# A fused diffusion layer on one core: the order of stores, casts and copies around the merged projections, changed in five places

## The chip, the core and the metric

The kernel runs on one core of a Trainium2 chip. The core has a matrix engine (TensorE, here PE; its weight loads are listed as PEld), three engines for elementwise work (VectorE, DVE; ScalarE, ACT; GpSimd, POOL) and SyncE (SP), which here only issues DMAs. POOL issues DMAs too. Each engine runs its own instructions in order and waits for the others by semaphores. The metric is the time of one execution on the device in microseconds, the median over runs.

## What is computed

One layer over 1024 latent tokens of width 1024, with 256 context tokens that only give the start states of a linear-attention scan. The reference, cut to what the change touches:

```
def project(h, w_in, w_a_up, b_a):
    z = h @ w_in
    q, k, v, g, lr_f, lr_b, u, bg, cg, r_gla, r_conv = jnp.split(z, offs, axis=-1)
...
def token_mixer(proj, grid_rows, s0_f, s0_b, gla_norm_g, gla_w_o, conv_w, conv_w_out, merge_w_out):
    o = o_f + flip_seq(o_b)                      # gated linear attention, two directions, 4 heads
    o = rms_norm(o, gla_norm_g).transpose(0, 2, 1, 3).reshape(bsz, n, GLA_DV).astype(dt)
    y_gla = (o * jax.nn.silu(g)) @ gla_w_o
    cu = cg * u
    conv = centred_conv3(cu.reshape(bsz, grid_rows, GRID_W, CONV_CH), conv_w).reshape(bsz, n, CONV_CH)
    y_conv = (bg * conv) @ conv_w_out
    merged = jax.nn.sigmoid(r_gla) * y_gla + jax.nn.sigmoid(r_conv) * y_conv
    return merged @ merge_w_out, s_f, s_b
...
    x = x + gt1 * y
    h = modulate(rms_norm(x, norm2_g[i]), sh2, sc2)
    x = x + gt2 * expert_choice_ffn(h, router_w[i], exp_w_gate[i], exp_w_up[i], exp_w_down[i])
return rms_norm(x, final_g)
```

The layer is followed by nothing else: 16 experts, each of which picks 128 of the 1024 tokens, take the second half of the time.

## The kernel before, in words

Matrices are in fp32, and a product of two of them is made of three matmuls in the engine's faster fp32r form: each operand is split into a high part (a cast on ACT, L75, names ending in h or hi) and a low part (a subtraction on DVE, L76, names ending in l or lo). In `mmw` (L88 is its matmul) the high and mixed terms of all rows come first, the terms with the weights' low part last.

**Heads and gates.** For each of four heads the kernel computes decays, values, queries and keys, and the scan (`head_core`, a generator), whose steps stand between the blocks of gate products (`gates`: four weights of two blocks each; ACT's sigmoid on L736 writes the block as `sgm`, and POOL stores it). The head's output `o` (two tiles) is then normed: DVE scales its eight pieces in place (L829), PE transposes them (L750, 16 of 128x128 a head), ACT copies the result (`ogs`, L752), and POOL stores it in `og_d`. This is `scale_store`. It is put on a list, `late`, and run in the next head behind its first values; for the last head it runs after the first of two weights of u products (`pu0`, two blocks each). `lm` makes the modulation of the second half meanwhile on DVE and PE (L768, L775). After `pu0` the pools of this part are closed, and the pools of the next part take over their space.

**Pairs.** The input projections u, cg, bg and g, two weight blocks of 128 columns at a time, are 15 "pairs" (`pair`; the first u is `pu0`): 2x2 blocks of weights and of tokens multiplied by seven products instead of eight, so that some operands are sums. A product is 12 matmuls into one PSUM bank; running sums are built up in the banks and copied out in between (`keep`, which calls `snap`, ACT, L953; 59 such copies). The token sums come from `tokens_split`: SP loads 16 pieces `yq` from DRAM (L869), four to a step k; each step has DVE's four sums (L879 and behind it) and two splits, and later two splits more, t3 and t4, the latter into the place of the old tokens. The weight sums come from `weights_side`, four steps to a pair: `whole(a)`, `whole(s_)`, then the differences, then `w3`; `whole` writes `whi` and `wlo` (three buffers each, the same ones that the gates' weights use). The pairs run u, cg, bg in turn (the first is cg), then four of G. `finish` of a cg pair adds, multiplies with u, and starts the conv over rows of 64: a multiply by the centre tap on ACT (L1052, `cv`) and two multiply-adds on DVE (L1054 is the first). `finish` of a bg pair multiplies and stores in `cv_d`. `finish` of a G pair takes the silu on ACT, multiplies by the head output loaded from `og_d` (`ot`) on DVE (L1077), and POOL stores it (L1078).

**Order.** From the token splits to the end of the last pair the order on PE, ACT and DVE is that of the code (`tc.manual_schedule`). What is to be done beside the products stands in a list `behind`: `prod` issues its 12 matmuls and then everything on that list, in the order in which it was put there. So a finish that was put there before a snapshot runs ahead of it on ACT. DMA queues (SP, POOL) and all that lies outside the stretch are ordered by the framework's scheduler, as is the program before it.

**Behind the pairs.** `cv_load` brings the conv rows back (16 tiles `cvt`, on POOL, L1089, from `cv_d`, each split into `cvh` and `cvl`): four ahead of the last pair, the others behind it, a load and its split at a time. The products with conv_w_out (24 matmuls each, `w` from a stream, operands `cvh`, `cvl`) follow the last pair at once. `t2_` tiles (128x512) of snapshots, `ot`, `cvt`, `cv`, `u` and `yq` share 14 buffers. The list `behind` is emptied like this:

```
        def prod(p, a, b, first=True):
            mmw(p, [(A[a](k), tk(b)(k)) for k in range(4)], 0, first, True, not first)
            for f in behind[:]:
                f()
            behind.clear()
```

Of the kernel before, what the change touches and what calls it, by code (L numbers as in the profile page):

```python
# [8 lines left out]
F32 = mybir.dt.float32  # L9
# [6 lines left out]
OP = mybir.AluOpType  # L16
# [19 lines left out]
def block_kernel(ctx: ExitStack, tc, x, c, cx, c_ctx, w_ada, b_ada, norm1_g, norm2_g, w_in, w_a_up, b_a,  # L36
# [717 lines left out]

    mod_d = dram.tile([4, D], F32, name="mod_d")
# [25 lines left out]
    for h in range(H):  # L781
# [6 lines left out]
        for t2 in range(0 if h else 2, 4):  # L788
            if t2 == 2:
                vt[1] = g4("v1")  # L790
            value_block(wv, vt, t2)
            drain(hd, 1)
            if t2 == 0 and late:
                late.pop()()
            if h:
                drain(lm, 1)
# [22 lines left out]
        drain(core, 1)  # L819
        while not drain(gt, 1):  # L820
            drain(core, 1)
            drain(lm, 1)
        drain(core)
        rs = small.tile([128, NCH], F32, name="rs_o", tag="rs_o")
        rstd_of(rs, ssq, DV, NCH)
        def scale_store(f, h=h, o=o, rs=rs):
            for t in range(4 * f, 4 * f + 4):
                os_ = o[f][:, (t % 4) * 256:(t % 4 + 1) * 256]
                V.tensor_scalar(os_, os_, rs[:, t:t + 1], None, op0=OP.mult)  # L829
            og_store(h, o, f)  # L830

        late.append(lambda f_=scale_store: (f_(0), f_(1)))
# [3 lines left out]
    for i in range(2):  # L836
        w = ws.get()
        for f in range(2):
            pu0[i, f] = p = ps()
            mmw(p, [(w(k), hs(k, f * 512, (f + 1) * 512)) for k in range(KT)])  # L840
        if late:
            late.pop()()
# [97 lines left out]
    def pair(n, finish, t_first=False):  # L940
# [4 lines left out]
        def prod(p, a, b, first=True):  # L945
            mmw(p, [(A[a](k), tk(b)(k)) for k in range(4)], 0, first, True, not first)
            for f in behind[:]:
                f()
            behind.clear()

        def snap(p, name="snap"):
            t = t2_(name)
            S.copy(t, p)  # L953
            return t

        def later(f):
            behind.append(f)

        def step():
            later(lambda: drain(nxt_, 1))  # L960
# [3 lines left out]
        def keep(n_, p):  # L964
            later(lambda: t.update({n_: snap(p)}))

        b1, b2, b3 = ps(), ps(), ps()
        if not t_first:
# [15 lines left out]
            later(lambda: finish(0, 1, b3, t["u2"]))  # L984
            prod(b1, (2, 2), (0, 1), False)
            step()
            later(lambda: finish(1, 0, b1, None))
# [6 lines left out]
        prod(b1, "s3", 3, False)  # L994
        prod(b2, (1, 1), (0, 0))
        keep("p1", b2)
        prod(b3, "s4", (1, 1), False)

# [21 lines left out]
    w0 = weights_side(0, ops[0])  # L1020
    drain(ts, 4)
    drain(w0, 1)
# [24 lines left out]
    def fin_cg(jp):  # L1047
        def finish(i, f, p, s_):
# [3 lines left out]
            S.activation(cvt, u, AF.Copy, scale=vcol("conv", 8 + j))  # L1052
# [12 lines left out]
    def fin_g(jp):  # L1065
# [5 lines left out]
        def finish(i, f, p, s_):  # L1071
            if s_ is not None:
                V.tensor_tensor(s_, p, s_, op=OP.add)
                p = s_
            sg = s_ if s_ is not None else t2_("sgg")
            S.activation(sg, p, AF.Silu)
            V.tensor_tensor(sg, sg, ot[i, f], op=OP.mult)  # L1077
            nc.gpsimd.dma_start(og2_d[2 * jp + i, :, f * 512:(f + 1) * 512], sg)  # L1078
# [4 lines left out]
    def cv_load():  # L1083
        for f in range(2):
            for g in range(2):
                hi, lo = cvT[g][f] = (Y("cvh"), Y("cvl"))
                for k in range(4):
                    t = t2_("cvt")
                    nc.gpsimd.dma_start(t, cv_d[4 * g + k, :, f * 512:(f + 1) * 512])  # L1089
                    split(hi[:, k * 512:(k + 1) * 512], lo[:, k * 512:(k + 1) * 512], t)  # L1090
                    yield
# [11 lines left out]
    for f in behind:  # L1103
        f()
# [655 lines left out]
```

## Time and profile before

| what | value |
| --- | --- |
| median of 3 runs | 2359.76 us (2357.66 to 2361.66) |
| profiled execution, its own time | 2357.01 us |
| its span in the profile | 2355.2 us (1.81 us lie around it) |
| PE busy | 2256.1 us, 96% |
| DVE busy | 1725.3 us, 73% |
| ACT busy | 1350.6 us, 57% |
| POOL busy | 281.2 us, 12% |
| heads and gates, u blocks | up to about 594 us |
| pairs | about 606 to 923 us |
| conv products, output products | from 923 us |

The page splits the span in 40 slices and gives PE's busy share in each: 9 tenths or more in 36 of them, 6 in the first, the fourteenth and the twenty-first, 7 in the last; its granted clock is at full speed in nearly all. Busy times are shares of one execution: an engine with 57% can still be the one that PE waits for at a certain place. The waits table names, for each idle stretch of an engine, what released it last. A timeline gives instructions by start time; several of one kind in a row are one row with their count. A matmul's time in such a row includes the end of its pipeline, so that neighbours overlap: the step from one start to the next is what it costs.

### The profile page before, as it was taken

Reading aid. Unit: us, or ns where it says so; the run is one execution under the profiler, and the core shown is the slowest. Engines: PE = TensorE matmul, PEld = TensorE weight load, DVE = VectorE, ACT = ScalarE, POOL = GpSimd, SP = SyncE. Lnnn points to the kernel's source line nnn. Section 1 sums busy time; section 2 is a strip of 40 time slices with the busy share of each in tenths; the row PEclk is TensorE's granted clock in tenths of the full one; section 3 lists DMA queues with packets and bytes.
Section 4 is the critical chain, followed back from the end, with each engine's and each line's share of the span. In section 5 each row is a group of like instructions: output and inputs, shape, how many; then the busy total and the mean of one; then the engine's idle time right before and its main releaser. Section 6 shows DMA issues by size and latency. Waiting matters only on the chain. (4 is left out here: it accounts for less than half of the span.)

```text
span 2355.2 us, 28981 instructions
## 1 busy us (share of the span) xinstructions
PE 2256.1 (96%) x10930; PEld 1866.7 (79%) x10930; DVE 1725.3 (73%) x2167; ACT 1350.6 (57%) x1554; POOL 281.2 (12%) x388
## 2 busy tenths in 40 slices
PE   6999999999699999999969999999999999999997
PEld 4888888888578777888748888888888888888885
DVE  5764545452855555458478999999999999999988
ACT  4744242422433334244328777778777777777786
POOL 1201010101000013420210110100111000011104
PEclk9999999999899999999989999999999999999998
DMA  9423333332322247765668999999999999999995
GB/s 324 147 69 109 109 104 101 116 93 86 101 68 66 72 139 232 242 192 168 254 224 310 374 379 377 384 389 389 385 380 380 386 373 399 386 387 383 375 349 212
DMA packets 356342, 589.60 MB, mean 250 GB/s; under 512 B 15499, under 2 KB 122097, under 8 KB 356201
## 3 DMA queue, kind: packets, MB, share of 16 engines
q1 hardware_dynamic: 331664, 506.65, 60.2%
q0 software_dynamic: 24192, 80.86, 10.3%
q8 instruction: 85, 1.39, 0.2%
q14 instruction: 57, 0.46, 0.1%
q10 hardware_dynamic: 344, 0.24, 0.0%
HBM read 537.34 MB, written 50.35 MB: 250 GB/s over the span
## 5 line engine op out<-in xcount | busy, mean ns | idle before, releaser
L76 DVE TENSOR_TENSOR ewl<-eraw,ewh 128x2048 fp32r<-128x2048 f32 (+1 forms) x391 | 865.2, 2222 | 93.6 <-ACT ewh L75 89.8
L75 ACT CAST ewh<-eraw 128x2048 fp32r<-128x2048 f32 (+1 forms) x391 | 726.7, 1862 | 224.0 <-PE ps L88 220.2
L88 PE MATMUL ps<-ewh,xeh 128*128 128x512 f32 x1024 | 404.5, 395 | 0.3 <-ACT xeh L75 0.3
L88 PE MATMUL ps<-ewh,xel 128*128 128x512 f32 x1024 | 399.8, 390 | 0.0
L88 PE MATMUL ps<-ewl,xeh 128*128 128x512 f32 x1024 | 274.0, 389 | 0.0
L88 PE MATMUL ps<-ewh,hd 128*128 128x512 f32 x1024 | 259.7, 396 | 0.0
L88 PE MATMUL ps<-hTh,whi 128*128 128x512 f32 x596 | 239.1, 401 | 11.9 <-ACT whi L75 11.9
L88 PE MATMUL ps<-hTl,whi 128*128 128x512 f32 x596 | 233.3, 391 | 0.0
L88 PEld LDWEIGHTS ps<-ewl,xeh 128*128 128x128 f32 x1024 | 192.2, 188 | 40.3
L88 PEld LDWEIGHTS ps<-ewh,xeh 128*128 128x128 f32 x1024 | 192.8, 188 | 39.3 <-ACT xeh L75 0.7
L88 PEld LDWEIGHTS ps<-ewh,xel 128*128 128x128 f32 x1024 | 192.9, 188 | 38.9 <-DVE xel L76 0.2
L88 PEld LDWEIGHTS ps<-ewh,hd 128*128 128x128 f32 x1024 | 189.7, 189 | 37.9
L75 ACT CAST whi<-wraw 128x1024 fp32r<-128x1024 f32 (+1 forms) x97 | 87.6, 917 | 155.9 <-PE ps L88 119.6
L76 DVE TENSOR_TENSOR wlo<-wraw,whi 128x1024 fp32r<-128x1024 f32 (+1 forms) x97 | 101.3, 1057 | 90.3 <-ACT whi L75 46.6
L88 PE MATMUL ps<-hTh,wlo 128*128 128x512 f32 x596 | 153.0, 391 | 0.0
L88 PEld LDWEIGHTS ps<-hTh,whi 128*128 128x128 f32 x596 | 112.7, 189 | 39.9 <-ACT whi L75 12.3
L88 PE MATMUL ps<-ewl,hd 128*128 128x512 f32 x512 | 137.4, 390 | 0.0
L1637 POOL DMA_INDIRECT x_d<-ye,idc x15 | 50.7, 3382 | 693.2 <-DVE ye L1636 693.2
L88 PEld LDWEIGHTS ps<-hTh,wlo 128*128 128x128 f32 x596 | 112.0, 189 | 23.7
L88 PEld LDWEIGHTS ps<-hTl,whi 128*128 128x128 f32 x596 | 112.7, 189 | 22.4
L88 PEld LDWEIGHTS ps<-ewl,hd 128*128 128x128 f32 x512 | 96.4, 188 | 20.5
L953 ACT COPY snap<-ps 128x512 f32<-128x512 f32 x59 | 34.5, 585 | 84.9 <-PE ps L88 84.9
(464 smaller groups left out, 3558.8 us busy)
## 6 DMA issues: line engine op xcount, KB each, us to landing
eraw<-in_exp_w_down_dram SPq DMA_DIRECT2D x128, 1024.0 KB
eraw<-in_exp_w_gate_dram SPq DMA_DIRECT2D x127, 1024.0 KB
eraw<-in_exp_w_up_dram SPq DMA_DIRECT2D x127, 1024.0 KB
wraw<-in_w_in_dram SPq DMA_DIRECT2D x76, 512.0 KB
raw<-in_w_ada_dram SPq DMA_DIRECT2D x64, 256.0 KB
adaw<-in_w_ada_dram SPq DMA_DIRECT2D x16, 512.0 KB
sig_d<-sgm POOLq DMA_DIRECT2D x32, 256.0 KB, 2.5
sgl<-sig_d POOLq DMA_DIRECT2D x32, 256.0 KB, 5.3
```

What stands on the lines that cost most here:

```text
L75: S.copy(hi, src)
L76: V.tensor_sub(lo, src, hi.bitcast(F32))
L88: T.matmul(p, a, b, start=first and i == 0, stop=last and i == len(seq) - 1, skip_group_check=again)
L953: S.copy(t, p)
L1637: nc.gpsimd.indirect_dma_start(out=x1_d[:, :], out_offset=bass.IndirectOffsetOnAxis(ap=idc[:, :1], axis=0), in_=ye, in_offset=None, comput ...
```

## The change

1. `scale_store` becomes a generator, `head_out`: the norm's factors and the scaling in its first steps, then the store of one output tile a step. For heads 0 to 2 it runs where it ran. For the last head, once its scan is done, it is drained a step at a time between the gate blocks, and what is left right behind them, before the u products.
2. The first step of the first pair's `weights_side` (`whole(a)`) stands ahead of the four token steps instead of behind them.
3. `behind` holds pairs of a delay and an action: `prod` issues those whose delay is 0, snapshots (delay -1) first, and counts the others down. `finish(0, 1)` and `finish(1, 0)` of all but the last pair get a delay of one product. The conv's centre-tap multiply goes from ACT to DVE.
4. In the G pairs `finish` only does the sum and the silu; the multiply and the store (`rest`) run behind the following product.
5. `cv_load` issues, from the fifth row on, up to four loads ahead of the row that it splits; in the last pair two steps of it (two splits, with their loads) run behind each of three products, so that 10 of 16 rows are split within the pairs' stretch.

The core of the diff:

```
+    def head_out(h, o, ssq):
+        rs = small.tile([128, NCH], F32, name="rs_o", tag="rs_o")
+        rstd_of(rs, ssq, DV, NCH)
+        yield
+        for f in range(2):
+            for t in range(4 * f, 4 * f + 4):
+                os_ = o[f][:, (t % 4) * 256:(t % 4 + 1) * 256]
+                V.tensor_scalar(os_, os_, rs[:, t:t + 1], None, op0=OP.mult)
+            if f == 0:
+                yield
+        for f in range(2):
+            og_store(h, o, f)
+            yield
...
         drain(core, 1)
+        outs = head_out(h, o, ssq)
         while not drain(gt, 1):
-            drain(core, 1)
+            if drain(core, 1) and h == H - 1:
+                drain(outs, 1)
             drain(lm, 1)
         drain(core)
...
+        drain(outs, 1)
+        late.append(outs)
+    drain(late.pop())
     drain(lm)
...
             mmw(p, [(w(k), hs(k, f * 512, (f + 1) * 512)) for k in range(KT)])
-        if late:
-            late.pop()()
...
             mmw(p, [(A[a](k), tk(b)(k)) for k in range(4)], 0, first, True, not first)
-            for f in behind[:]:
-                f()
-            behind.clear()
+            now = [q for q in behind if q[0] <= 0]
+            behind[:] = [(d - 1, f) for d, f in behind if d > 0]
+            for d, f in sorted(now, key=lambda q: q[0]):
+                more = f()
+                if callable(more):
+                    behind.append((0, more))
...
         def keep(n_, p):
-            later(lambda: t.update({n_: snap(p)}))
+            later(lambda: t.update({n_: snap(p)}), -1)
...
-            later(lambda: finish(0, 1, b3, t["u2"]))
+            later(lambda: finish(0, 1, b3, t["u2"]), 1)
...
-            later(lambda: finish(1, 0, b1, None))
+            later(lambda: finish(1, 0, b1, None), 1)
...
         prod(b1, "s3", 3, False)
+        later(lambda: drain(cl, 2) and None, 1)
         prod(b2, (1, 1), (0, 0))
         keep("p1", b2)
+        later(lambda: drain(cl, 2) and None)
         prod(b3, "s4", (1, 1), False)
+        later(lambda: drain(cl, 2) and None, 1)
...
+    drain(w0, 1)
     drain(ts, 4)
-    drain(w0, 1)
...
-            S.activation(cvt, u, AF.Copy, scale=vcol("conv", 8 + j))
+            V.tensor_scalar(cvt, u, vcol("conv", 8 + j), None, op0=OP.mult)
...
-            V.tensor_tensor(sg, sg, ot[i, f], op=OP.mult)
-            nc.gpsimd.dma_start(og2_d[2 * jp + i, :, f * 512:(f + 1) * 512], sg)
+            def rest():
+                V.tensor_tensor(sg, sg, ot[i, f], op=OP.mult)
+                nc.gpsimd.dma_start(og2_d[2 * jp + i, :, f * 512:(f + 1) * 512], sg)
+            return rest
...
+        todo, got = [(f, g, k) for f in range(2) for g in range(2) for k in range(4)], {}
+        for i, (f, g, k) in enumerate(todo):
+            for f_, g_, k_ in todo[i:i + (1 if i < 4 else 5)]:
+                if (f_, g_, k_) not in got:
+                    got[f_, g_, k_] = t = t2_("cvt")
+                    nc.gpsimd.dma_start(t, cv_d[4 * g_ + k_, :, f_ * 512:(f_ + 1) * 512])
```

**The last head's output, on PE.** Before, around its transposes (L750, `o_4325` and `o_4326` are the two output tiles; `whi`, `wlo` ahead of them belong to the first u weights, behind them to the second; a number of a token tile `hTh`, `hTl` is a row block):

```order
L88 MATMUL ps<-hTh_685,wlo 128x512 x2
L88 MATMUL ps<-hTh_687,wlo 128x512 x2
L88 MATMUL ps<-hTh_689,wlo 128x512 x2
L750 MATMUL ps<-ident,o_4325 128x128 x8
L750 MATMUL ps<-ident,o_4326 128x128 x8
L88 MATMUL ps<-hTh_683,whi 128x512
L88 MATMUL ps<-hTl_684,whi 128x512
```

Now, in the last gate's first block, ahead of and behind whose first twelve matmuls they stand:

```order
L88 MATMUL ps<-hTh_685,wlo 128x512 x2
L88 MATMUL ps<-hTh_687,wlo 128x512 x2
L88 MATMUL ps<-hTh_689,wlo 128x512 x2
L750 MATMUL ps<-ident,o_4325 128x128 x8
L88 MATMUL ps<-hTh_683,whi 128x512
L88 MATMUL ps<-hTl_684,whi 128x512
```

and twelve matmuls later:

```order
L88 MATMUL ps<-hTh_687,whi 128x512
L88 MATMUL ps<-hTl_688,whi 128x512
L750 MATMUL ps<-ident,o_4326 128x128 x8
L790 MATMUL ps<-acc,ones 1x512
L88 MATMUL ps<-hTh_689,whi 128x512
L88 MATMUL ps<-hTl_690,whi 128x512
```

The 16 transposes moved from between the two u weights to the last gate, the second eight just ahead of the small matmul of the modulation (L790, before L775).

**ACT at the same place**, where `sgm` are the gates' sigmoids, `ogs` the copies of the transposed output, the last `whi` the first pair's weights and `t1h` the first token split. Before:

```order
L736 ACTIVATE sgm<-ps 128x512
L75 CAST whi<-wraw 128x1024
L736 ACTIVATE sgm<-ps 128x512 x3
L752 COPY ogs<-ps 128x512 x4
L75 CAST t1h<-yq 128x512
```

Now:

```order
L736 ACTIVATE sgm<-ps 128x512
L75 CAST whi<-wraw 128x1024
L736 ACTIVATE sgm<-ps 128x512
L752 COPY ogs<-ps 128x512 x4
L736 ACTIVATE sgm<-ps 128x512
L75 CAST whi<-wraw 128x1024
L736 ACTIVATE sgm<-ps 128x512
L75 CAST t1h<-yq 128x512
```

The copies come two sigmoids earlier, and the cast `whi` stands ahead of the token splits; before, it stands behind all of them.

**ACT from the first cg pair into the bg pair behind it**, where `snap` are snapshots (L953, now L965), `cv` the conv's centre-tap multiplies and `whi`, `w_5214` casts of weights. Before:

```order
L953 COPY snap<-ps 128x512
L75 CAST whi<-wraw 128x1024
L1052 ACTIVATE cv<-u,vec 128x512
L953 COPY snap<-ps 128x512 x2
L75 CAST whi<-s_5142 128x1024
L953 COPY snap<-ps 128x512
L75 CAST whi<-wraw 128x512 x2
L1052 ACTIVATE cv<-u,vec 128x512 x2
L75 CAST w_5214<-wraw 128x512
L1052 ACTIVATE cv<-u,vec 128x512
L953 COPY snap<-ps 128x512
```

Now:

```order
L965 COPY snap<-ps 128x512
L75 CAST whi<-wraw 128x1024
L965 COPY snap<-ps 128x512 x2
L75 CAST whi<-s_5142 128x1024
L965 COPY snap<-ps 128x512
L75 CAST whi<-wraw 128x512 x2
L75 CAST w_5214<-wraw 128x512
L965 COPY snap<-ps 128x512
```

The `cv` rows are gone from ACT, and the last snapshot stands right behind the weights' cast.

**POOL in the last pair**, where `og_d<-snap` and `og_d<-sgg` are stores of G's results, `cvt<-cv_d` the loads of conv rows and `sgl<-sig_d` the first load of what comes behind. Before:

```order
L1078 DMA og_d<-snap 128x512
L1078 DMA og_d<-sgg 128x512 x2
L1089 DMA cvt<-cv_d 128x512 x2
L1078 DMA og_d<-snap 128x512
L1078 DMA og_d<-sgg 128x512
L1089 DMA cvt<-cv_d 128x512 x2
L1078 DMA og_d<-snap 128x512
L1089 DMA cvt<-cv_d 128x512 x8
L1132 DMA sgl<-sig_d 128x512
```

Now:

```order
L1188 DMA gt_7780<-mod_d 128x1024
L1096 DMA og_d<-snap 128x512 x2
L1096 DMA og_d<-sgg 128x512
L1109 DMA cvt<-cv_d 128x512 x10
L1096 DMA og_d<-sgg 128x512
L1109 DMA cvt<-cv_d 128x512 x2
L1096 DMA og_d<-snap 128x512
L1096 DMA og_d<-sgg 128x512
L1156 DMA sgl<-sig_d 128x512
```

Ten of the loads stand in one row behind one store, two behind the next; before, they stood two, two and eight behind three places in the stores.

## Rows read from the trace of the kernel before

**Rows 1.** Waits of PE, whole span: engine, tile, line <- releaser: us, times, longest.
```profile
PE ps L88 <- ACT snap L953: 17.3, 5, 5.3
PE ps L88 <- ACT whi L75: 11.9, 1, 11.9
...
PE ps L88 <- ACT cvh L75: 4.1, 3, 2.1
```

**Rows 2.** Busy time by stretch; columns: stretch, us, busy by engine (instructions), PEclk, DMA share, GB/s.
```profile
core 0: us, PE busy (x) PEld busy (x) DVE busy (x) ACT busy (x) POOL busy (x), PEclk, DMA share, GB/s
678.20:697.24 19.04, 19.04 (x86) 15.77 (x85) 10.88 (x16) 7.32 (x11) 0.00 (x0) 1.00 0.21 55
697.24:721.18 23.94, 20.94 (x85) 16.86 (x84) 15.68 (x23) 7.95 (x12) 0.54 (x1) 0.93 0.20 55
1500.00:1550.00 50.00, 50.00 (x235) 41.41 (x234) 46.05 (x30) 38.85 (x30) 5.93 (x2) 1.00 1.04 379
```

**Rows 3.** PE's timeline, first pair: start, us, line, operation, out<-in, count, [idle <-releaser].
```profile
561.04 1.02 PE L775 MATMUL ps<-acc,ones 128*1 128x512 f32 x2
...
568.48 1.98 PE L88 MATMUL ps<-hTh,wlo 128*128 128x512 f32 x8
...
581.18 1.91 PE L750 MATMUL ps<-ident,o 128*128 128x128 f32 x16
...
592.01 1.98 PE L88 MATMUL ps<-hTh,wlo 128*128 128x512 f32 x8
...
619.04 0.79 PE L88 MATMUL ps<-t2h,whi 128*128 128x512 f32 x1 [5.27 <-ACT snap L953]
```

**Rows 4.** SP's timeline at the token loads, same columns.
```profile
583.12 12.70 SPq L869 DMA_DIRECT2D yq<-y_d  x16
```

**Rows 5.** DVE's timeline from the last head's scaling to the first pair.
```profile
554.76 2.19 DVE L829 TENSOR_SCALAR o<-o,rs_o 128x256 f32<-128x256 f32 x8
...
589.36 0.69 DVE L879 TENSOR_TENSOR yq<-yq 128x512 f32<-128x512 f32 x1 [26.58 <-DMA yq<-y_d]
...
605.50 0.68 DVE L884 TENSOR_TENSOR yq<-yq 128x512 f32<-128x512 f32 x1
606.11 1.22 DVE L76 TENSOR_TENSOR wlo<-wraw,whi 128x1024 fp32r<-128x1024 f32 x1
```

**Rows 6.** ACT's timeline, first cast over the old tokens, and the first pair's first snapshot.
```profile
606.71 0.62 ACT L75 CAST hTh<-yq 128x512 fp32r<-128x512 f32 x1
...
618.40 0.58 ACT L953 COPY snap<-ps 128x512 f32<-128x512 f32 x1
```

**Rows 7.** PE's timeline from the first cg pair to the last pair.
```profile
639.73 1.07 PE L88 MATMUL ps<-hTh,wlo 128*128 128x512 f32 x4
643.79 0.50 PE L88 MATMUL ps<-t2h,whi 128*128 128x512 f32 x1 [3.00 <-ACT snap L953]
...
902.49 1.07 PE L88 MATMUL ps<-hTh,w 128*128 128x512 f32 x4
```

**Rows 8.** ACT's timeline at the first of the four late snapshots.
```profile
642.55 0.72 ACT L1052 ACTIVATE cv<-u,vec 128x512 f32<-128x512 f32 x1 [2.28 <-DVE u L1045]
643.18 0.57 ACT L953 COPY snap<-ps 128x512 f32<-128x512 f32 x1
```

**Rows 9.** DVE's group of a tensor-scalar, same shape: count | busy us, mean ns | idle.
```profile
L768 DVE TENSOR_SCALAR acc<-raw,cS 128x512 f32<-128x512 f32 x8 | 3.8, 474 | 0.0
```

**Rows 10.** DVE's waits for the conv multiply: us, times, longest.
```profile
DVE cv L1054 <- ACT cv L1052: 12.7, 16, 0.8
```

**Rows 11.** PE's timeline at the last pair's end and the conv products.
```profile
921.96 1.07 PE L88 MATMUL ps<-hTh,w 128*128 128x512 f32 x4
...
946.07 1.98 PE L88 MATMUL ps<-cvh,wlo 128*128 128x512 f32 x8
```

**Rows 12.** POOL's timeline in the last pair: its DMA issues.
```profile
910.15 0.54 POOL L1078 DMA_DIRECT2D og_d<-sgg  x1 [0.36 <-DVE sgg L1077]
919.93 0.54 POOL L1078 DMA_DIRECT2D og_d<-sgg  x1 [9.24 <-DVE sgg L1077]
```

**Rows 13.** Conv rows' tile, 880 to 960 us: its transfers from issue to landing.
```profile
DMA to landing us min/median/max: 4.8/5.9/7.5
```

More of the change, by code (lines that the diff above doesn't have):

```diff
@@ L819, in block_kernel @@
         drain(core, 1)
+        outs = head_out(h, o, ssq)
         while not drain(gt, 1):
-            drain(core, 1)
+            if drain(core, 1) and h == H - 1:
+                drain(outs, 1)
             drain(lm, 1)
         drain(core)
[L824 to L832, printed above, removed]
+        drain(outs, 1)
+        late.append(outs)
+    drain(late.pop())
     drain(lm)
@@ L840, in block_kernel @@
             mmw(p, [(w(k), hs(k, f * 512, (f + 1) * 512)) for k in range(KT)])
-        if late:
-            late.pop()()
     close(hp)
@@ L954, in snap, with later @@
             return t
-        def later(f):
-            behind.append(f)
+        def later(f, d=0):
+            behind.append((d, f))
         def step():
-            later(lambda: drain(nxt_, 1))
+            later(lambda: drain(nxt_, 1) and None)
         t = {}
         def keep(n_, p):
-            later(lambda: t.update({n_: snap(p)}))
+            later(lambda: t.update({n_: snap(p)}), -1)
         b1, b2, b3 = ps(), ps(), ps()
@@ L1083, in cv_load @@
     def cv_load():
-        for f in range(2):
-            for g in range(2):
-                hi, lo = cvT[g][f] = (Y("cvh"), Y("cvl"))
[L1087 to L1091, printed above, removed]
+        todo, got = [(f, g, k) for f in range(2) for g in range(2) for k in range(4)], {}
[4 more added lines that the diff above has]
+                    nc.gpsimd.dma_start(t, cv_d[4 * g_ + k_, :, f_ * 512:(f_ + 1) * 512])
+            if k == 0:
+                hi, lo = cvT[g][f] = (Y("cvh"), Y("cvl"))
+            split(hi[:, k * 512:(k + 1) * 512], lo[:, k * 512:(k + 1) * 512], got[f, g, k])
+            yield
     def cv(k, f):
@@ L1102, in block_kernel @@
         pair(n, {O_U: fin_u, O_CG: fin_cg, O_BG: fin_bg, O_G: fin_g}[b_](jp), last_)
-    for f in behind:
-        f()
+    while behind:
+        more = behind.pop(0)[1]()
+        if callable(more):
+            behind.append((0, more))
     order.__exit__(None, None, None)
```

## The prediction

> **What bounds the kernel now.** I read the table of waits of TensorE (PE) first: PE works in nearly all of the span, and an engine that PE doesn't wait for costs nothing. Of its waits three lie where the diff works [rows 1]: 17.3 us in five waits for a snapshot (the copy of a product's running sum from PSUM by ScalarE, ACT), 11.9 us in one wait for a weight cast, 4.1 us in three waits for the conv rows' cast. A wait is not the whole loss, so next I read PE's busy time and granted clock by pairs: an undisturbed pair takes 19.04 us, all of it busy, at clock 1.00; one with a 3 us wait takes 23.94 at 0.93 [rows 2]. The first gives the rate: seven products of 12 matmuls, 2.72 us each, 0.227 a matmul. Each loss below is a stretch's length less its matmuls at that rate, so wait and slow restart together. Last I read what comes behind: in the experts PE is busy 50.00 of 50 us at clock 1.00, VectorE (DVE) 46, ACT 39 [rows 2]. PE sets that stage, and its loads start when buffers come free, so what is saved ahead of it should move it forward whole.
>
> **Term 1, the start of the pairs.** PE ends the last gate at 570.29 (eight matmuls from 568.48), does 16 transposes at 581.18 between the two blocks of u weights, and ends the second block at 593.82 (eight from 592.01) [rows 3]. Then come 11.9 us of wait, two products at a slow clock, 5.27 us of wait, and the third product at 619.04 [rows 1, 3]. Followed back: the third product waits for the snapshot of the first, which on ACT stands behind the casts of the split tokens. These come from four token steps on DVE, 589.36 to 606.18 (16.8 us); the first began when its tiles had landed, 6.2 us after SyncE (SP) issued the loads at 583.12, and SP issued them when the last transposes were done [rows 3 to 5]. The first pair's weight cast stands behind the token steps: its low part on DVE began only at 606.11 [rows 5].
>
> The change takes both apart. The transposes go into the last gate, whose first block starts at 558.3 (twelve matmuls before 561.04 [rows 3]). Their input, the scaled output, is ready at 554.76 + 2.19 = 556.95 [rows 5], ahead of that, so I cost the move at nothing but the transposes' own 1.66 us: the gates end at 571.95, and the u blocks are shorter by as much. The two eights stand twelve matmuls apart and so end at 558.3 + 0.83 + 2.72 + 0.83 = 562.7. SP can issue from 563, 20 us earlier, and the first tiles land at 569.2. The first pair's cast reuses the buffer that the last gate reads until 571.95; its low part takes 1.23 on DVE [rows 5]: 573.2. The four token steps follow, 573.2 + 16.8 = 590.0. One of the split results overwrites tokens that the second u block still reads, so its first cast waits for the first of the last eight matmuls, about 592.4. From that cast to the end of the snapshot the trace has 606.71 to 618.98, 12.27 us [rows 6]; so the snapshot ends at 604.7, and the third product starts at 604.8 instead of 619.04: **14.2 us**. Meanwhile PE does products 1 and 2 straight on from 593.82 and waits once, about 5.5 us; the slow restart behind that I leave as it is. Bounds: if the tokens came no earlier, only the 1.2 us of the weights' low part would leave the chain. If the 12.27 us shrank until nothing waits, 619.04 - 593.82 less two products is 19.8, and the restart of some 2.5 us would go too: 22.3. I take 14.2, the sum of the rows above.
>
> **Term 2, the snapshots.** From 639.73 to 902.49, the last four matmuls of a product each, the trace has 89 products in 262.76 us [rows 7], where 89 x 2.72 are 242.08. The loss is **20.7 us**, four losses of about 5 us, one in each pair that follows a cg pair. Each begins with a 3.00 us wait for a snapshot [rows 7]; these four and the 5.27 are the 17.3 of [rows 1]. ACT shows why: the snapshot ran at 643.18, behind a conv multiply at 642.55 that itself had waited 2.28 us for DVE's u [rows 8]. Its product had ended at 637.9, one product before the end of the next at 640.6 (four matmuls from 639.73). The change removes the queue: the snapshot stands first behind its product, the two costly finishes go one product later, and the conv multiply leaves ACT. Ahead of it on ACT stays one weight cast; it should run within a microsecond of its product's end, some 2 us before it is needed. I take all 20.7; the least, if these waits stay, is 0.
>
> What pays is DVE, with 16 multiplies more. The nearest row is a tensor-scalar of the same shape, 474 ns [rows 9], so 7.6 us; against it DVE no longer waits for ACT's multiply, 12.7 us in 16 waits [rows 10]. Over a cg pair and the bg pair behind it DVE is busy 10.88 + 15.68 = 26.6 us [rows 2], with four multiplies 28.5, in 38.1 us of PE. The finishes bunch, though: counted into the cg pair alone, weights and four finishes make about 20 us against 19.04, a lag of 1 us that the bg pair makes good. PE needs nothing of DVE within that microsecond. I cost it at nothing; if that cover is gone, snapshots and casts come late again, which is the first rival.
>
> **Term 3, the last pair and the conv rows.** From 921.96 to 946.07 PE does 4 + 24 + 24 + 16 matmuls [rows 11], 15.42 us at the rate above, in 24.11: 8.69 are lost to conv rows that come late. GpSimd (POOL) issues their loads behind stores: the store at 919.93 had waited 9.24 us for DVE, and loads stand right behind it [rows 12]. A load lands 5.9 us after its issue [rows 13], then comes the split, 1.3. The change puts ten loads in a row behind an earlier store (910.15 [rows 12]), so at about 911, and the pair's last product inside the first conv product. What stays: that product needs DVE's sums, 0.8 us late by my count, and the last two rows stand behind a store whose multiply DVE ends near 928: 928.1 + 0.5 + 5.9 + 1.3 = 935.8. In PE's order 22 matmuls come between 928.3 (the end of the first conv product) and the use of these rows, so 933.3, or 934.1 with the 0.8. That is 0.8 and 1.7 of wait; the first falls where the product has matmuls ahead of it, so I take 1.7 for both, 1.5 of slow clock behind it, and gain 8.7 - 3.2 = **5.5 us**. Bounds: 8.7 with all on time, 2 if the last rows lose as much as now; below nothing if the loads don't overlap (third rival).
>
> The Trainium skill, "DMA: Bandwidth & Descriptors", section "Anatomy of one DMA — SWDGE (gpsimd) path", puts such a transfer at about 2.0 us plus its bytes at 436 GB/s; for 256 KB that gives an estimate of 2.6 us. The trace's median is 5.9 and its shortest 4.8 [rows 13], so the page is too low here, and the trace's duration stands. By the page the last rows would land 3.3 us sooner, term 3 would be about 7.2, and the time 2317.7.
>
> The G pairs' multiply and store, which run one product later, cost nothing: their readers come after the conv products, over 20 us behind.
>
> **Sum.** 14.2 + 20.7 + 5.5 = 40.4. The profiled run took 2357.0 (span 2355.2 and 1.8 around it): 2316.6. The median of the runs is 2.75 above it, so **2319.4 us** on the median.
>
> **Rivals.** *The snapshots stay late.* If DVE falls behind in the cg pair and ACT's weight cast waits for it with the snapshot behind it, the four losses remain: 2319.4 + 20.7 = 2340. For it: 20 us against 19.04. Against: the lag is 1 us, the snapshot has 2, and the bg pair has room. 0.07.
>
> *The tokens don't come earlier.* SP waits for the last reader of the space that the tokens take. If that is the last gate's output, stored near 574, the tiles land at 580 and 7 of the 14.2 are lost: 2326. If the chain keeps its place altogether, term 1 is its lower bound: 2332. For it: the trace shows only the last reader, not the next to last. Against: none of the outputs in that space is held longer than the transposes in the code. 0.06.
>
> *The loads ahead run one by one: slower.* The last pair's tiles share 14 buffers (4 outputs, 3 snapshots, the conv rows). If only one is free at a time, twelve loads at 5.9 + 1.3 = 7.2 us take 86.4, from 911 to 997.4, where PE wants the last at 933.3: 64 late, of which 8.7 are lost already. 55.4 against 34.9 gained makes 2380. It decides from 5.5 us a load on, with fewer than about 1.3 in flight. For it: the buffers of three of the ten loads are last read by DVE, late in the pair. Against: the other seven are free by then. 0.05.
>
> *The gain is lost behind.* The DMA share is 1.04 in the experts [rows 2]; if the weights came at a rate fixed from the start, time saved ahead would come back as waits: 2360. Against: PE never waits there. 0.04.
>
> **How the numbers follow.** Forecast 0.78; rivals 0.07, 0.06, 0.05, 0.04. The range: low 2311, term 1 at its upper bound (8.1 more); high 2336, the second rival's 2332.4 with term 3 at its lower bound (3.5 less). Outside lie the first, third and fourth rival, 0.16, and a rest. Faster by over 0.2% (4.7 us, about what a measurement of this kernel can tell from no change): 0.91; same 0.04; slower 0.05.
>
> **What would show it.** SP's token loads should start near 563, not 583; the third product near 605; PE's waits for snapshots should fall from 17.3 to about 6, without the 3.00 us ones; its 11.9 us wait for the first cast and DVE's waits for the conv multiply should be gone; the loss at the conv rows should be about 3. Wrong would be: token loads past 575; a lag of DVE that grows from pair to pair, with waits for low parts in place of snapshots; conv loads over 2 us apart; new waits of PE in the experts.

## The result, and the profile after

The changed kernel takes **2316.51 us** (median of 4 runs, 2315.55 to 2319.61) against 2358.71 of the kernel before (4 runs, 2357.08 to 2361.66); the ratio is 0.9822, with a 95% interval from 0.9805 to 0.9839. The forecast was 2319.4, in a range from 2311 to 2336.

The profiled execution after took 2319.61 us, span 2317.8. It is the longest of its four, and it lost time ahead of anything that the change touches. The first long sequence of matmuls that waits for nothing any more are the context states; their third group stands here in PE's timeline, first before, then after (start, duration, line, operation):

```profile
150.80 0.59 PE L548 MATMUL ps<-vc,kdc 128*128 128x256 f32 x2
```

```profile
154.99 0.59 PE L548 MATMUL ps<-vc,kdc 128*128 128x256 f32 x2
```

By there this execution is 4.19 us later. It is late by that much after its first 50 us already, in code that is the same in both: 1.7 us of it are longer waits for the first loads and casts, and the rest is mostly slow matmuls (the work from 28.5 to 47.3 us took 18.85 us at a granted clock of 0.91, before 17.25 at 1.00). In all executions below this mark lies between 149.2 and 155.3, and this spread at the start is of the size of the spread of the times. So places in two traces are compared from this mark: **scale of before** means a time after less 4.19.

The waits of PE over the whole span after (engine, tile, line, releaser: us, times, longest), those in the heads' end and the pairs:

```profile
PE ps L88 <- ACT snap L965: 5.3, 1, 5.3
...
PE ps L88 <- DVE cvl L76: 0.8, 1, 0.8
...
PE ps L88 <- DVE snap L1018: 0.6, 1, 0.6
```

Against [rows 1]: of 17.3 us for snapshots the 5.3 at the third product are left, the 11.9 us for the first weight cast are gone, and of the 4.1 us for the conv rows' cast nothing is left; 0.8 for a conv row's low part and 0.6 for a sum stand in that place.

**Term 1** in the same order as [rows 3 to 6]: PE, SP, DVE and ACT at the start of the pairs.

```profile
562.44 1.03 PE L750 MATMUL ps<-ident,o 128*128 128x128 f32 x8
...
566.05 1.03 PE L750 MATMUL ps<-ident,o 128*128 128x128 f32 x8
567.02 1.02 PE L790 MATMUL ps<-acc,ones 128*1 128x512 f32 x2
...
608.93 0.79 PE L88 MATMUL ps<-t2h,whi 128*128 128x512 f32 x1 [5.27 <-ACT snap L965]
```

```profile
567.12 15.10 SPq L878 DMA_DIRECT2D yq<-y_d  x16
```

```profile
576.57 1.23 DVE L76 TENSOR_TENSOR wlo<-wraw,whi 128x1024 fp32r<-128x1024 f32 x1 [7.82 <-PE ps L88]
577.72 0.69 DVE L888 TENSOR_TENSOR yq<-yq 128x512 f32<-128x512 f32 x1
...
593.26 0.69 DVE L893 TENSOR_TENSOR yq<-yq 128x512 f32<-128x512 f32 x1
```

```profile
596.68 0.62 ACT L75 CAST hTh<-yq 128x512 fp32r<-128x512 f32 x1 [3.05 <-PE ps L88]
...
608.30 0.58 ACT L965 COPY snap<-ps 128x512 f32<-128x512 f32 x1
```

On the scale of before SP issues the token loads at 562.9 (583.12 before), the first pair's low part runs at 572.4, the token steps from 573.5 to 589.8, the first cast over the old tokens at 592.5, and the third product starts at 604.74: 14.3 us earlier than 619.04.

**Term 2.** The two rows of PE that answer to 639.73 and 902.49 in [rows 7] lie 242.08 us apart, which is 89 x 2.72 to the hundredth. No product in between waits:

```profile
629.67 1.07 PE L88 MATMUL ps<-hTh,wlo 128*128 128x512 f32 x4
...
871.75 1.07 PE L88 MATMUL ps<-hTh,w 128*128 128x512 f32 x4
```

The same cg pair and bg pair as in [rows 2], now both of 19.04 us, at clock 1.00 (columns as there):

```profile
663.22:682.26 19.04, 19.04 (x86) 15.77 (x84) 11.37 (x17) 6.71 (x10) 0.00 (x0) 1.00 0.21 55
682.26:701.30 19.04, 19.04 (x86) 15.77 (x84) 17.15 (x26) 6.16 (x9) 0.54 (x1) 1.00 0.25 70
```

DVE has 28.5 us to do in the two, as forecast (10.88 + 15.68 + 1.9), but the order puts more of it into the bg pair than I had counted: 11.37 in the cg pair, 17.15 behind.

**Term 3.** PE at the last pair's last product and the conv products, then POOL's issues:

```profile
893.79 0.50 PE L88 MATMUL ps<-cvl,whi 128*128 128x512 f32 x1 [0.84 <-DVE cvl L76]
894.12 0.87 PE L88 MATMUL ps<-cvh,wlo 128*128 128x512 f32 x3
895.59 0.51 PE L88 MATMUL ps<-hTh,w 128*128 128x512 f32 x1 [0.60 <-DVE snap L1018]
...
908.63 1.98 PE L88 MATMUL ps<-cvh,wlo 128*128 128x512 f32 x8
```

```profile
882.47 0.54 POOL L1096 DMA_DIRECT2D og_d<-sgg  x1
883.00 2.67 POOL L1109 DMA_DIRECT2D cvt<-cv_d  x5
886.46 1.13 POOL L1109 DMA_DIRECT2D cvt<-cv_d  x2 [0.79 <-DMA og_d<-snap]
890.67 0.54 POOL L1109 DMA_DIRECT2D cvt<-cv_d  x1 [3.08 <-DVE cvl L76]
891.94 0.54 POOL L1109 DMA_DIRECT2D cvt<-cv_d  x1 [0.74 <-DVE cvl L76]
894.03 0.54 POOL L1109 DMA_DIRECT2D cvt<-cv_d  x1 [1.55 <-DVE cvl L76]
899.00 0.55 POOL L1096 DMA_DIRECT2D og_d<-sgg  x1 [4.43 <-DVE sgg L1095]
899.54 1.07 POOL L1109 DMA_DIRECT2D cvt<-cv_d  x2
```

From 871.75 to 908.63 PE takes 36.88 us for the matmuls that took 43.58 before (902.49 to 946.07): **6.7 us** less. The matmuls alone are 34.46, so 2.4 us are still lost. The last two rows, which I had expected late, are on time. The ten loads follow each other in the queue, as the order above has them, but they don't go out at once: five do, two come after a short wait for a store, and the last three one by one, each held until DVE has split an earlier row.

From the mark to 908.63 the changed kernel is 41.6 us faster (14.3, 20.7 and 6.7, but for rounding); less the 4.2 of the later start that is 37.4, which is the difference of the two profiled times (2357.01 - 2319.61). Behind 908.63 nothing moves against the kernel before: the spans differ by the same 37.4. In the experts PE is busy throughout (columns as in [rows 2]):

```profile
1500.00:1550.00 50.00, 50.00 (x232) 41.39 (x231) 45.39 (x30) 39.69 (x33) 2.56 (x1) 1.00 1.04 395
```

### The profile page after: what moved, and what is told of

Same layout as the page of the kernel before. It is cut to its first block, busy times and chain, and to the rows that moved or that the text cites. A ratio compares the mean times of both kernels' runs of the same rounds, so it can differ in the third digit from the quotient of the medians.

```text
span 2317.8 us, 28964 instructions
## 1 busy us (share of the span) xinstructions
PE 2243.7 (97%) x10930; PEld 1861.4 (80%) x10930; DVE 1734.1 (75%) x2183; ACT 1341.3 (58%) x1538; POOL 281.8 (12%) x388
## 5 line engine op out<-in xcount | busy, mean ns | idle before, releaser
L965 ACT COPY snap<-ps 128x512 f32<-128x512 f32 x59 | 34.7, 589 | 100.2 <-PE ps L88 96.3
```

## Experiments

The theory: three causes that don't touch each other, each with one edit that removes it (early stores; the conv multiply off ACT; conv rows loaded ahead), and everything behind is set by PE. The rivals: that the other edits (cast first, delays and sorting, the later multiply and store) are needed too, and that loads ahead can serialize. Edits are shown against the kernel named. Times are medians, the kernel before on the same chip beside them.

### Early stores alone

```
-            drain(core, 1)
+            if drain(core, 1) and h == H - 1:
+                drain(outs, 1)
```

(the kernel before, with `head_out` in the place of `scale_store`)

> The kernel before with part 1 alone (last head's outputs stored between its gates); the first pair's cast still stands behind the token steps. Theory: the early token loads alone make term 1. The token steps then start when the tiles land (about 569 to 573 on the scale of the profile before), end near 590, the first pair's low part follows by 591.5, still ahead of the u blocks' end at 593.8; third product near 605, 14 us saved, time about 2344.5 with before at 2358.7. PE's 11.9 us wait for the weight cast is gone although the cast wasn't moved; the four 3.00 us waits stay. Rival: both parts are needed, since the cast behind the token steps keeps PE waiting; then the wait for the cast stays at several us and under 9 us are saved (2350 or more).

2344.75 us against 2359.05; ratio 0.9934, interval 0.9918 to 0.9951. PE's waits from 600 us to 940:

```profile
PE ps L88 <- ACT snap L962: 17.3, 5, 5.3
PE ps L88 <- ACT cvh L75: 4.3, 2, 3.4
```

The 11.9 us for the weight cast are gone without moving the cast, and the third product starts at 608.32 with the mark at 154.43, so 14.3 us earlier. The early stores make all of term 1; the cast behind the token steps is still early enough.

### Cast first alone

```
-    drain(ts, 4)
     drain(w0, 1)
+    drain(ts, 4)
```

> The kernel before with part 2 alone (first pair's weights cast ahead of the token steps). Theory: the token chain keeps its place, products 1 and 2 run straight on behind the u blocks, and the wait moves whole to the third product: one wait of about 18 us for the snapshot in place of 11.9 + 5.3, third product near 617.8, 1.2 us saved, 2357.5. Rival: the cast is what starts the chain, and moving it saves 5 us or more (2353 or less).

2357.98 us against 2359.05; ratio 0.9993, interval 0.9983 to 1.0003. The one wait, from PE's timeline:

```profile
621.66 0.80 PE L88 MATMUL ps<-t2h,whi 128*128 128x512 f32 x1 [18.66 <-ACT snap L953]
```

The mark is at 154.33 here, so the third product stands at 618.1 on the scale of before, where the forecast of the theory was 617.8. Two waits, 11.88 and 5.27 us, have become one of 18.66. It is 1.5 us longer than the two, since the first two products, which ran at a granted clock of 0.70 behind the first wait, now take their 5.4 us at 1.00. What is left is 0.9 us at the third product, near the lower bound of term 1; the times can't tell it from nothing. A wait that is removed ahead of a later one on the same chain is not saved.

### The conv multiply on DVE alone

```
-            S.activation(cvt, u, AF.Copy, scale=vcol("conv", 8 + j))
+            V.tensor_scalar(cvt, u, vcol("conv", 8 + j), None, op0=OP.mult)
```

> The kernel before with one line of part 3: the conv's centre-tap multiply on DVE; no delays, snapshots not sorted ahead. Theory: the queue in front of the late snapshots was this multiply, waiting for DVE's u; without it the snapshot runs right behind the weight cast, the four 3.00 us waits go, 20.7 us saved, 2338. Rival: the snapshots need to be sorted first and the finishes to be delayed, since DVE, with 7.6 us more to do, gets late with the next weights' sums, and ACT's casts and the snapshot wait for these; then half or less is saved (2348 or more).

2338.26 us against 2359.05; ratio 0.9913, interval 0.9897 to 0.9930. PE's waits from 600 us to 940:

```profile
PE ps L88 <- ACT whi L75: 11.9, 1, 11.9
PE ps L88 <- ACT snap L953: 5.4, 1, 5.4
PE ps L88 <- ACT cvh L75: 4.1, 2, 2.4
PE ps L88 <- DVE cvl L76: 0.2, 1, 0.2
```

One line saves 20.8 us, the whole of term 2. The four waits of 3.00 us are gone with no delay and no sorting.

### The conv multiply back on ACT in the changed kernel

The same line, the other way round, in the changed kernel.

> The changed kernel with the conv's centre-tap multiply back on ACT; delays and sorted snapshots stay. Theory (the mirror of the run above): the multiply stands behind the snapshot now, so the snapshot is on time, but a multiply that waits for DVE still blocks the weight casts behind it; I expect PE to wait a little in cg and bg pairs, 0 to 5 us lost against the changed kernel, 2316.5 to 2321.5. Rival: the multiply on ACT is what costs, wherever it stands: 15 us or more lost, 2332 or more.

2318.74 us against 2359.05; ratio 0.9833, interval 0.9816 to 0.9849. PE's waits from 500 us to 960:

```profile
PE ps L88 <- ACT snap L965: 5.3, 1, 5.3
PE ps L88 <- DVE snap L1018: 0.6, 1, 0.6
PE ps L88 <- DVE cvl L76: 0.5, 1, 0.5
```

These are the waits of the changed kernel. The time is 2 us above that of the changed kernel, but the mark is at 154.39, and the profiled 2318.03 less its 3.6 us are 2314.4 on the scale of before, where the changed kernel has 2315.4. So with the snapshots sorted ahead and the two finishes delayed, the multiply on ACT costs nothing that the trace shows: term 2 has two sufficient remedies, and the change contains both. Whether the sorting would do without the delays was not run.

### No loads ahead

```
         prod(b1, "s3", 3, False)
-        later(lambda: drain(cl, 2) and None, 1)
...
-            for f_, g_, k_ in todo[i:i + (1 if i < 4 else 5)]:
+            for f_, g_, k_ in todo[i:i + 1]:
```

(all three such `later` lines are left out)

> The changed kernel without part 5: conv rows loaded a row at a time, none of the 12 split within the last pair; the G pairs' multiply and store stay one product later. Theory: term 3 comes from the loads ahead; its loss at the conv products, 2.4 us in the changed kernel's trace, goes back to about 9 as before, 6.7 us lost, 2323. Rival: the later store does part of it (the last sums on DVE come sooner, so the loads do), and only 3 us or less are lost (2319.5 or less).

2323.13 us against 2358.96; ratio 0.9848, interval 0.9832 to 0.9865. It is 6.6 us above the changed kernel's 2316.51, and the third conv product's low part, counted from the mark, is later by the same 6.6. PE waits as before: 4.2 us in two waits for `cvh`. Term 3 comes from the loads ahead, with the splits inside the last pair that they allow, not from the later stores.

### One buffer for the conv rows

```
-                    got[f_, g_, k_] = t = t2_("cvt")
+                    got[f_, g_, k_] = t = cpool.tile([128, 512], F32, name="cvt", tag="c1", bufs=1)
```

(with loads one at a time, and 13 buffers for the other tiles)

> The changed kernel with one buffer of its own for the conv rows (a tag with one buffer; the others share 13), so that each load waits for the split of the row before. This is the third rival's mechanism built on purpose: 12 rows at 5.9 + 1.3, 7.2 us each with the issue. By the rival's sum the last row is used some 64 us late, and the time is 2319.4 + 55.4 + 5.5 = 2380, slower than before. If DMA and split overlap more than I think (a load lands nearer its shortest 4.8 and the split's buffer is free after its 0.7 on DVE), it comes to about 2365.

2355.39 us against 2358.96; ratio 0.9984, interval 0.9974 to 0.9995: 39 us above the changed kernel, but neither 2380 nor 2365. The loads do run one by one. Four of them, POOL's timeline, and below them the landing times of all between 850 and 960 us:

```profile
904.44 0.54 POOL L1109 DMA_DIRECT2D cvt<-cv_d  x1 [4.02 <-DVE cvl L76]
909.20 0.54 POOL L1109 DMA_DIRECT2D cvt<-cv_d  x1 [4.22 <-DVE cvl L76]
913.79 0.54 POOL L1109 DMA_DIRECT2D cvt<-cv_d  x1 [4.05 <-DVE cvl L76]
918.50 0.54 POOL L1109 DMA_DIRECT2D cvt<-cv_d  x1 [4.17 <-DVE cvl L76]
```

```profile
DMA to landing us min/median/max: 2.9/3.1/5.0
```

A row costs 4.7 us here, not 7.2, since these loads, with no other conv row beside them, land in about 3 us, not in the 5.9 of [rows 13]. Further on, between POOL's other loads, the steps are 5.1 to 6.6 us, and the last ten steps (899.87 to 951.64) take 5.2 on the mean. That is still under the 5.5 us a row from which the third rival made the kernel slower, and so even this extreme gives back nearly all of the gain but no more. With 5.2 in place of 7.2 the rival's sum says 37 us, an estimate, where 39 came. The mechanism of the rival is real, its price was too high. Its first sign is not at the conv products: in the last pair three casts of conv rows stand ahead of a snapshot on ACT, each waits 3.2 to 4.0 us for its load, and PE waits 12.4 us for the snapshot:

```profile
889.18 0.79 PE L88 MATMUL ps<-t3h,whi 128*128 128x512 f32 x1 [12.41 <-ACT snap L965]
```

### Multiply and store not delayed

```
-            def rest():
-                V.tensor_tensor(sg, sg, ot[i, f], op=OP.mult)
-                nc.gpsimd.dma_start(og2_d[2 * jp + i, :, f * 512:(f + 1) * 512], sg)
-            return rest
+            V.tensor_tensor(sg, sg, ot[i, f], op=OP.mult)
+            nc.gpsimd.dma_start(og2_d[2 * jp + i, :, f * 512:(f + 1) * 512], sg)
```

> The changed kernel without part 4: in the G pairs multiply and store stand right behind the silu again. Theory: DVE waits for the silu as before (6.3 us in 9 waits) but has room in the G pairs, so nothing is lost there; in the last pair DVE's sums and the splits come up to 1 us later, 0 to 2 us lost, 2316.5 to 2318.5. Rival: the splits of the conv rows now stand behind DVE's waits for ACT, and the conv loss goes to 6 or more: 2320 or more.

2315.33 us against 2358.96; ratio 0.9813, interval 0.9796 to 0.9829. Nothing is lost; PE's 0.84 us wait for a low part at the conv products is even gone, 0.6 us is the only wait left there. From the mark, the third conv product's low part stands 1 to 2 us earlier than in the two traces of the changed kernel. Part 4 is not needed, and may itself cost about 1 us.

### Three edits of the change alone

The changed kernel with the cast behind the token steps again, no delays, no sorting, no later store; early stores, multiply on DVE and loads ahead are left.

> The changed kernel reduced to three edits: early stores of the last head, the conv multiply on DVE, conv rows loaded ahead. Undone are the cast ahead of the token steps (part 2), the delays and the sorting of snapshots (rest of part 3) and the delayed multiply and store (part 4). Theory: these three carry all; within 2 us of the changed kernel, 2315 to 2318.5. Rival: the undone edits are needed once the others are in place (the multiply on DVE makes DVE late for the snapshots' neighbours); 5 us or more lost, 2321 or more.

2315.96 us (5 runs, 2314.85 to 2319.45) against 2358.92; ratio 0.9823, interval 0.9810 to 0.9836.

> The changed kernel itself, for comparison with the other two on one chip: 2316.5. In its profile the third product of the pairs should start 14.3 us earlier than before, counted from the first matmuls of the context states, and the conv products' third low part 41.6 us earlier.

The changed kernel beside it, on the same chip: 2316.32 us (2315.85 to 2317.70), ratio 0.9822, interval 0.9809 to 0.9835. Its third product stands at 606.58 with the mark at 152.62, 14.3 us earlier than before; the third conv product's low part is 42.5 us earlier, 0.9 more than in its first trace. The two can't be told apart by their times. In the three edits' trace PE has one wait more, 1.5 us for a snapshot (6.8 us in two waits for snapshots instead of 5.3 in one); it stands in the last pair. So one of the undone edits is worth something of that size at this place, below what the times show; which one was not run. The gains and losses of the single runs, 14.3, 20.8 and 6.6, add up to 41.7 of the 42.2 us: the three causes don't touch each other.

### What is left: the first pair

The 5.3 us wait at the third product is the largest left in the changed stretch. The snapshot that it waits for stands on ACT behind all casts of tokens and weights, and one of those waits 3.05 us for the u blocks (ACT at 596.68 above). Three versions reorder the first pair; the second and the third also undo part 4. The last one, without that part of its edit:

```
         for k in range(4):
             c_, t3, t4 = y[k]
             c_(3, t3)
+            yield
+        for k in range(4):
+            c_, t3, t4 = y[k]
             c_(4, t4)
             yield
...
     drain(w0, 1)
     drain(ts, 4)
+    drain(w0, 1)
     for (i, f), p in pu0.items():
+        if i and f:
+            drain(ts, 1)
+            drain(w0, 1)
         us[i, f] = t2_("u")
         S.copy(us[i, f], p)
-        drain(ts, 1)
-        if i or f:
-            drain(w0, 1)
+        if not (i and f):
+            drain(ts, 1)
...
             keep("p1", b1)
+            if n == 0:
+                later(lambda: drain(ts, 2) and None)
             prod(b2, (1, 2), (1, 0))
+            if n == 0:
+                later(lambda: (drain(ts, 2), drain(w0, 1)) and None)
```

> The changed kernel with the first pair reordered: only two of the four last token steps run ahead of the first pair's products, two behind its first snapshot, and the last two weight steps behind its second product. The wait of 5.27 us for the first snapshot remains in the changed kernel because the snapshot stands behind all token and weight casts on ACT. Theory: the snapshot then ends about 1 us behind its product, and the third product starts on time: 5.3 us of wait and some 2.4 us of slow clock saved, 7.7 in all, 2308.8. Rival: the casts that the fifth and sixth product need (third token sum, last token block) are now late instead, and the wait moves there: under 3 us saved, 2313.5 or more.

The first version keeps two token steps, with the cast that waits, ahead of the products: 2311.67 us against 2358.96; ratio 0.9796, interval 0.9780 to 0.9812. About 5 of the 7.7 us expected come; two waits of 1.10 and 1.37 us for snapshots appear at the fifth and the seventh product.

> The first pair's reordering once more: besides what the first version moved, the second and third snapshots stand ahead of the weight casts that aren't due yet, and the first finish of that pair comes three products later; part 4 is undone. Theory: in the first version the waits of 1.10 and 1.37 us for the second and third snapshot came from casts ahead of them on ACT that waited for DVE; with these behind the snapshots both go, with 1 to 2 us of slow clock: 3 us less than the first version, 2308.5. Rival: the late finish pushes DVE's work into the second pair, and the waits come there: no better than the first version, 2311 or more.

The second version moves the first finish three products back: 2313.92 us against 2358.92; ratio 0.9810, interval 0.9797 to 0.9824. No better than the first. PE's timeline shows where the wait went:

```profile
613.37 0.50 PE L88 MATMUL ps<-hTh,w 128*128 128x512 f32 x1 [1.41 <-ACT snap L965]
...
635.77 0.80 PE L88 MATMUL ps<-hTh,w 128*128 128x512 f32 x1 [3.08 <-ACT snap L965]
```

The first is in the first pair, the second in the second. There the snapshot ran at 635.14, behind a weight cast on ACT that had waited 6.31 us for DVE's sum:

```profile
634.19 1.04 ACT L75 CAST whi<-s 128x1024 fp32r<-128x1024 f32 x1 [6.31 <-DVE s L929]
```

DVE came to that sum at 633.41, behind the finishes of the first pair, which had begun only at 614.00. DVE's work was pushed into the pair behind, as the rival said.

> The first pair's reordering with the casts sorted by what they wait for: the weight sums and the third token sum, which wait for nothing, fill the time in which the u blocks end; the casts over the old tokens, which wait for these blocks, come behind the first snapshot; finishes as in the changed kernel; part 4 is undone. Theory: in the first version ACT and DVE stood about 3 us still behind one cast that waited for the u blocks, and what was late in that pair was late by that; without it all three waits for snapshots in the first pair go, 5.3 us and some 2.4 of slow clock against the changed kernel, 2308.6. Rival: ACT and DVE have more work in the first pair than fits (its own casts and the next pair's), whatever the order; then a wait of 2 to 4 us stays somewhere in the first or second pair and the time is 2311 or more.

The third version lets nothing stand behind a cast that waits for the u blocks: **2309.64 us** (5 runs, 2307.34 to 2311.36) against 2359.38; ratio 0.9789, interval 0.9775 to 0.9802, apart from the changed kernel's 0.9809 to 0.9835 of its 5 runs. Of the 6.7 us between the two medians about 1 may be the undone part 4. PE's waits from 600 us to 940, and the stretch of the first two pairs (columns as in [rows 2]):

```profile
PE ps L88 <- DVE snap L1025: 0.6, 1, 0.6
PE ps L88 <- ACT snap L968: 0.3, 1, 0.3
```

```profile
600.00:640.00 40.00, 40.00 (x176) 32.54 (x175) 35.69 (x53) 16.55 (x28) 1.08 (x2) 1.00 0.25 66
```

PE is busy in all of it, with DVE at 35.7 of 40 us. The work fits; it was its order that made PE wait.

## Why the prediction was right, and where it was off

**Where it was read from** was right: PE's table of waits named the three places, and what was saved ahead of the experts moved them whole: PE is busy 50.00 of 50 us there after the change too, and the spans' difference is that at the conv products. The fourth rival (gain lost behind) falls.

**Term 1**, 14.2 forecast, 14.3 measured; each step is within 0.4 us: the loads' issue at 562.9 for 563, the low part at 572.4 for 572.0, the steps' end at 589.8 for 590.0, the third product at 604.74 for 604.8. The one wait of 5.5 us is 5.27. The second rival (tokens no earlier) falls. What I had not separated is which edit does it: I told the weight cast as if both were needed, and the early stores alone gave 14.3 us. The lower bound, 1.2 for the cast alone, was right at about 1.

**Term 2**, 20.7 forecast, 20.68 measured; the reading of ACT's two rows [rows 8], a snapshot queued behind a multiply that waits for DVE, was the cause, as the one-line edit showed. My sentence on how it goes away listed three edits as if they worked together. Either the move to DVE or the sorting and the delays together do it, and the first alone gave all. The cost on DVE was nothing, as forecast; the first rival falls.

**Term 3**, 5.5 forecast, 6.7 measured, is the step that was mis-sized, by 1.2. Two terms of it were off. The residual was put at 3.2, 1.7 of wait and 1.5 of slow clock, and is 2.4: 0.84 and 0.60 of wait, and 1.0 in single steps longer than 0.227 us, most of them beside these waits. The slow clock that I had priced didn't come: the granted clock is 1.00 from 871.75 to 908.63, where it was 0.86 from 921.96 to 946.07 before. The 0.8 for DVE's sums was 0.60, but the other wait is not for the last two rows. It is 0.84 us for an earlier row's low part, behind a weight's low part on DVE. The last two rows were issued some 2 us later than I put it and still came in time, since they landed in 3.4 and 3.6 us (their casts run from 902.99) where I took 5.9. And the kernel before had lost 0.4 us more than I counted, ahead of 921.96 in the last pair.

**The third rival** was a mechanism that exists, with a price that came from the same 5.9: the one-buffer kernel gave 39 us over the changed one where the rival's sum said 61. A transfer's duration depends on what runs beside it; taken from a bunch it is too long for a lone one. One sign that I had named for being wrong, conv loads over 2 us apart, did appear in the changed kernel: the starts at 890.67 and 894.03 lie 3.7 and 2.1 us behind the load before. These loads were held back for DVE, three of ten, as the rival's text had put it, and neither of PE's two waits there is for one of their rows; so the sign was drawn too sharply.

**The weighing of the Trainium skill against the row** failed with it. I set the Trainium skill's "DMA: Bandwidth & Descriptors", section "Anatomy of one DMA — SWDGE (gpsimd) path", aside because the row said 5.9 against an estimate of 2.6 us from that page. Loads without another conv row beside them, in the one-buffer kernel, land in 2.9 to 5.0 us, median 3.1, near that estimate, so the Trainium skill and the row don't disagree; they tell of different loads, and for the last two rows the Trainium skill was the nearer. The variant of the sum by its estimate, 7.2 for term 3, is off by 0.5, the one I took by 1.2; part of that nearness is luck, since the variant has neither the wait of 0.84 us nor the 0.4 us ahead of 921.96.

**The whole**: 40.4 forecast, 41.6 measured from the mark, 42.2 between the medians. The median itself, forecast at 2319.4, came out 2.9 lower; 1.05 of that is the median of before, which a fourth run moved from 2359.76 to 2358.71.

## What to carry to other kernels

Before an engine is given more or less work, look at what stands in its queue ahead of the instruction that the bound engine waits for, and at what that one waits for itself: one line's multiply on the wrong engine cost 20.7 us, with a busy time of 0.7 us for each of its 16. Of several waits on one chain only the last counts, so price each edit with the others absent; here three edits carried everything. Where work of two engines must fit beside a third, sort it by what it waits for, and put what waits for the bound engine last.

## What the runs showed of the hardware

The same load of 256 KB, issued by POOL, landed in 3.1 us (median) when no other conv row was under way; four in a row took 4.6 to 4.9 in the changed kernel, five in a row 5.9 to 6.4, and eight in a row 5.6 to 7.5 in the kernel before. The program's first 60 us differ from run to run, by waits for first loads and by the granted clock: the mark at the context states lay between 149.2 and 155.3 us in the traces, while from there to the end the changed kernel's two traces took equal time to within 1.4 us. A wait of 3.00 us for a snapshot cost PE 4.7 to 6.1 us in all, since the matmuls behind it ran at a lower granted clock (0.85 to 0.93 in the 22 to 23 us around each); two waits of 0.84 and 0.60 us left the clock at 1.00.
